# Decoder layer: three output tiles of the projection's middle part issued behind attention's last value product, and other slots for the last part's loads

## The chip, the cores and the metric

One core of a Trainium2 chip runs the whole program. Its engines work side by side, each in its own order: TensorE (PE in the profile, its weight loads PEld), VectorE (DVE), ScalarE (ACT), GpSimd (POOL) and SyncE (SP), which issues most DMAs. The metric is device time in microseconds of one execution; a median over several runs is given.

## The reference

One layer of a causal decoder, for 1024 prompt tokens and 8 sequences of 8 new tokens (N = 1088 columns, D = 1024):

```python
h = rms_norm(x, norm_mix_g)
proj = h @ w_in                       # conv branch a, and q, k, v of 12 heads of 64
a = silu(layer_norm(depthwise_conv(glu(proj)), ...))          # width 31
o = attend(q, k, v)                   # dilated windows (128,1), (512,4), (2048,16), merged
x = x + concatenate([a, o]) @ w_out   # the output projection: 1024 x 1024
h = rms_norm(x, norm_ffn_g)
x = x + (silu(depthwise_conv(h @ w_gate)) * (h @ w_up)) @ w_down
y = rms_norm(x, norm_final_g)
```

Outputs are y for prompt and new tokens, the keys and values, and the convolution states. All of it is float32; the change touches the line of `w_out` and what stands before and behind it.

## The kernel before

Activations lie with channels on the 128 partitions and the 1088 tokens along the free side, so that an operand is eight tiles of 128 x 1088. Every float32 factor is split in a high part (rounded by a ScalarE copy) and a low part (the difference, by VectorE or GpSimd), and a product is three matmuls: high x high, high x low, low x high (`gemm`, L188 to L190; `block_product`, L951 to L954).

**Order of the work.** A planner simulates the engines while the program is built and writes each engine's order: of the instructions that are ready in its simulation, the one that stands first in the program is taken. `tc.issue_after(ins)` binds an instruction behind another one on the same engine, without a wait on any other engine; `high_priority` moves instructions forward. On the chip each engine follows its written order strictly, so one that waits holds up all behind it. SyncE's DMA queue is such an order too.

**Attention.** `prompt_heads` goes through the 12 heads, each in two halves `u`. `scores` (L673 matmuls, L677 masks and row minima on VectorE) is followed by `weighted` of the half before: exponentials (L714, ScalarE), transposes of the weights (L741, into two PSUM banks `t`, copied to SBUF at L745 and L747), and value products (L762) that sum in one PSUM tile `o`; they stand in the list `done`. L765 copies one half of the result; `turned_out[0]` is that copy. `normalise` ends a pair of heads: sums are exchanged (L651), turned (L778) and multiplied (L780, the tile `cat`), and stored to DRAM in `mixed`. The cached sequences go through `sample_attention` in between.

**Output projection in three parts.** `PARTS = (3, 3, 2)` splits the 1024 input channels. The first part (conv branch and the first attention tile) and the middle part (three attention tiles) are `out_part`: for each of eight output tiles m, weights are loaded (`load_w`: raw load L157, high part L161 on ScalarE, low part L163 on GpSimd; two raw buffers, five buffers for parts), `gemm` runs over the three input tiles, and the result is added to `x2[m]` (L890, VectorE) from two PSUM banks. TensorE takes these matmuls wherever attention leaves it free. `ORDER = (4, 5, 6, 7, 0, 1, 2, 3)` and `DEFER = 3`: for tiles 4, 5 and 6 the middle part makes only the first 544 columns, and the other 544 are deferred to the last part.

**The last part.** It contracts the last two attention tiles, in two column halves of 544 (`out_half(0)`, `out_half(1)`), with four PSUM pairs of two banks. Its memory is the pool F, laid over the pools of attention and of the parts before; each tag of F has eight slots of 544 columns, and a load into a slot waits for the readers of what lay there. Its loads run in one chain on SyncE (`queued` and `load_input`, each behind `last_load`), its ScalarE conversions in one chain behind `turned_out[0]` (`last_high`). Before the change the loads come in this order: input 0 of half 0, raw weights of four output tiles (two loads), input 0 of half 1, raw weights of the other four, weights of the three deferred tiles, four raw gate weights, the three deferred inputs, input 1 of half 1, four raw up weights. Input 1 of half 0 is not loaded but made from `cat` in SBUF (L921, L922). The low parts of half 1's two inputs are made on VectorE (L1016), all others by GpSimd (L1003), and `lows_made` keeps the last of them: the first residual add (L1174), and through it all others of half 0, is issued behind it. Each tile of half 0 is one product of 12 matmuls of 272 columns; then its residual add, a store to DRAM (L1176), a square (L1179) and the sum of squares (L1183). Half 1 does the deferred product too for its first three tiles. Then come the norm, the scaling (L1188) and the first products of the feed-forward net, which holds the time from about 605 us to the end.

## Time and profile before

| | us |
|---|---|
| median of 3 runs | 1336.86 (1335.79 to 1343.06) |
| profiled execution | 1336.84 |
| its span, first to last instruction | 1335.1 |
| TensorE busy in the span | 1293.8 |
| VectorE, ScalarE, GpSimd busy | 936.4, 561.0, 472.5 |
| mean granted TensorE clock | 0.989 |

The span is what the profile shows of one execution. "Busy" of TensorE counts its pipelined matmuls, each until its end, so starts of successive matmuls lie closer than their durations. The granted clock is the share of full speed that the throttle allowed. Times in rows count from the span's start. A row of a timeline gives start, length, engine, line, operation, operands, and in brackets the idle time before it with what ended it.

### The profile page before, as it was taken

The numbers are of one execution on the slowest core, as the hardware profiler recorded it, in microseconds if no ns is written. First come the engines' busy times: TensorE is split into PE (matmuls) and PEld (weight loads), VectorE is DVE, ScalarE is ACT, GpSimd is POOL, SyncE is SP. The second block draws the span as 40 slices with busy tenths as digits, with TensorE's granted clock in tenths as the row PEclk, the third lists the DMA queues.
The fourth block names the chain that finished last, engine by engine and source line by source line (L and its number), as shares of the span: only waits on it lengthen the run. The fifth ranks groups of instructions, "written<-read, shape, count | busy, mean of one in ns | idle before, by whom it ended". The sixth has DMA issues, their size and how long they took to land.

```text
span 1335.1 us, 26004 instructions
## 1 busy us (share of the span) xinstructions
PE 1293.8 (97%) x10322; PEld 1253.4 (94%) x10322; DVE 936.4 (70%) x1793; ACT 561.0 (42%) x1130; POOL 472.5 (35%) x387
## 2 busy tenths in 40 slices
PE   9999999999999999889999999999999999999996
PEld 9999988999978879788999999999999999999996
DVE  7478879565575677468977677676776659967656
ACT  7321221547584564454633233333333344334432
POOL 0121112111011125321647556464565544445610
PEclk9999999999999999889999999999999999999999
DMA  9248677564799985351023231332313395352412
GB/s 328 59 169 290 245 268 206 166 167 118 216 285 290 311 273 161 102 209 47 32 91 123 91 122 48 108 122 91 121 35 121 100 356 194 108 180 92 156 41 95
DMA packets 93658, 211.43 MB, mean 158 GB/s; under 512 B 13920, under 2 KB 42720, under 8 KB 93536
## 3 DMA queue, kind: packets, MB, share of 16 engines
q1 hardware_dynamic: 92960, 209.02, 47.8%
q8 instruction: 81, 1.33, 0.4%
q10 hardware_dynamic: 576, 0.75, 0.2%
q14 instruction: 41, 0.34, 0.1%
HBM read 153.69 MB, written 56.04 MB: 157 GB/s over the span
## 4 chain that ended last, share of the span: by engine, by line
PE 83%; DVE 10%; DMA 4%; issue 2%; ACT 0%; SPq 0%; DVEq 0%; ACTq 0%
PE g L188 6%; PE g L190 6%; PE g L189 6%; PE g L951 5%; PE g L954 5%; PE g L953 5%; PE py L951 5%; PE py L953 5%; PE py L954 4%; PE px L954 3%; PE pz L953 3%; PE pz L951 3%; PE pz L954 3%; PE px L953 3%; PE px L951 3%; PE s L673 3%
## 5 line engine op out<-in xcount | busy, mean ns | idle before, releaser
L163 POOL TENSOR_TENSOR wl<-wr,wh 128x1024 fp32r<-128x1024 f32 (+1 forms) x34 | 60.1, 1769 | 307.2 <-PE g L190 175.5
L188 PE MATMUL g<-xh,wh 128*128 128x384 f32 (+1 forms) x472 | 157.0, 333 | 1.3 <-DVE qkv L469 0.7
L190 PE MATMUL g<-xh,wl 128*128 128x384 f32 (+1 forms) x472 | 155.4, 329 | 0.0
L189 PE MATMUL g<-xl,wh 128*128 128x384 f32 (+1 forms) x472 | 155.3, 329 | 0.0
L951 PE MATMUL g<-ux,as 128*128 128x272 f32 x504 | 145.2, 288 | 0.4 <-DVE x L1584 0.4
L954 PE MATMUL g<-ux,as 128*128 128x272 f32 x504 | 145.4, 289 | 0.0
L953 PE MATMUL g<-ux,as 128*128 128x272 f32 x504 | 144.8, 287 | 0.0
L1102 POOL TENSOR_TENSOR wb<-wr,wb 128x512 fp32r<-128x512 f32 x79 | 115.0, 1465 | 54.0 <-ACT wb L1101 54.0
L1494 POOL TENSOR_TENSOR as<-ar,as 128x640 fp32r<-128x640 f32 (+1 forms) x56 | 92.1, 1654 | 101.4 <-ACT as L1493 90.5
L1101 ACT ACTIVATE wb<-wr 128x512 fp32r<-128x512 f32 x79 | 49.6, 628 | 160.6 <-DVE wr L1136 102.9
L951 PEld LDWEIGHTS g<-ux,as 128*128 128x128 f32 x504 | 95.1, 189 | 0.8 <-issue 0.8
L954 PEld LDWEIGHTS g<-ux,as 128*128 128x128 f32 x504 | 94.9, 188 | 0.0
L953 PEld LDWEIGHTS g<-ux,as 128*128 128x128 f32 x504 | 94.7, 188 | 0.0
L714 ACT ACTIVATE y<-y,m 128x128 f32<-128x128 f32 (+1 forms) x192 | 88.5, 465 | 12.4 <-DVE m L702 11.5
L188 PEld LDWEIGHTS g<-xh,wh 128*128 128x128 f32 x472 | 88.8, 188 | 3.7 <-issue 2.1
L1362 DVE SCALAR_TENSOR_TENSOR fc<-gb,prm,fc 128x1104 f32<-128x1104 f32 x44 | 80.5, 1851 | 14.8 <-ACT fc L1360 14.4
L189 PEld LDWEIGHTS g<-xl,wh 128*128 128x128 f32 x472 | 88.9, 188 | 0.2
L190 PEld LDWEIGHTS g<-xh,wl 128*128 128x128 f32 x472 | 88.9, 188 | 0.0
L415 DVE SCALAR_TENSOR_TENSOR cacc<-gp,prm,cacc 128x1024 f32<-128x1024 f32 x60 | 85.0, 1416 | 0.1
L1102 POOL TENSOR_TENSOR wa<-wr,wa 128x512 fp32r<-128x512 f32 x40 | 54.6, 1366 | 79.4 <-ACT wa L1101 79.4
L677 DVE CUSTOM_DVE_ANT_0 y<-s,pmk 128x128 f32<-128x128 f32 (+1 forms) x192 | 63.7, 376 | 26.1 <-PE s L673 23.4
L161 ACT ACTIVATE wh<-wr 128x1024 fp32r<-128x1024 f32 (+1 forms) x36 | 29.6, 822 | 116.2 <-PE g L190 91.9
(399 smaller groups left out, 4316.6 us busy)
## 6 DMA issues: line engine op xcount, KB each, us to landing
cr<-in_kc SPq DMA_DIRECT2D x24, 768.0 KB, 8.3
cr<-in_vc SPq DMA_DIRECT2D x24, 768.0 KB, 7.9
ux<-ub SPq DMA_DIRECT2D x63, 272.0 KB, 4.0
kk<-dk SPq DMA_DIRECT2D x48, 256.0 KB, 5.6
wr<-in_w_in SPq DMA_DIRECT2D x20, 512.0 KB, 5.4
wr<-in_w_gate SPq DMA_DIRECT2D x20, 512.0 KB, 3.3
wr<-in_w_up SPq DMA_DIRECT2D x20, 512.0 KB, 4.5
ub<-u SPq DMA_DIRECT2D x18, 544.0 KB, 3.7
```

Of the source, the lines that this page charges most:

```text
L188: nc.tensor.matmul(ps[c], whi[:, k, :], xh[:, t0:t0 + n], start=(k == 0), stop=False)
L189: nc.tensor.matmul(ps[c], whi[:, k, :], xl[:, t0:t0 + n], start=False, stop=False)
L190: nc.tensor.matmul(ps[c], wlo[:, k, :], xh[:, t0:t0 + n], start=False, stop=(k == nk - 1))
L415: eng.scalar_tensor_tensor(acc[:, :S], gp[:, j:j + S], col(w0 + j), acc[:, :S], op0=ALU.mult, op1=ALU.add)
L677: nc.vector.tensor_tensor_reduce(out=y[:, o:o + n], in0=ps[:, o:o + n], in1=mask, op0=ALU.add, op1=ALU.min, scale=1.0, scalar=3e38, accum_ ...
L714: nc.scalar.activation(y, y, AF.Exp, bias=m[:, 4 * g + i:4 * g + i + 1], scale=-1.0, accum_out=den[:, g, 2 * hd + u, i:i + 1])
L951: nc.tensor.matmul(ps, whi[:, k, :], xh[:, t], start=(start and k == 0), stop=False, skip_group_check=True)
L953: nc.tensor.matmul(ps, whi[:, k, :], xl[:, t], start=False, stop=False, skip_group_check=True)
L954: last = nc.tensor.matmul(ps, wlo[:, k, :], xh[:, t], start=False, stop=(stop and k == nk - 1), skip_group_check=True).ins
L1102: nc.gpsimd.tensor_sub(lo, x, hi.bitcast(F32))
L1362: nc.vector.scalar_tensor_tensor(c[:, :W], gb[i][:, t:t + W], col(C_FW + 3 * f + t), c[:, :W], op0=ALU.mult, op1=ALU.add)
L1494: nc.gpsimd.tensor_sub(lo, raw, hi.bitcast(F32))
```

## The change

- `weighted` keeps its last value product in `weighed[0]`. In the middle part, the matmuls of output tiles 5, 6 and 7 (`m >= KT - BEHIND`) are issued behind it; the evictions are not bound.
- The last part's raw weights are loaded into slots of tag `b11` in place of `t1`; the low parts of these weights go to `t3` in place of `b21`, except the first pair's.
- The three deferred inputs are loaded (and converted) ahead of the deferred tiles' weights and the gate weights, and their raw and low tile lies in `b21`, in place of `t3`.
- `lows_made` is gone. The two low parts of half 1's inputs are kept in `late_lows` and made on VectorE behind the third and the fourth residual add of half 0, and the first residual add of a half is bound to nothing.

```diff
+BEHIND = 3
@@ weighted
                             done.append(nc.tensor.matmul(dst, v, m, start=first, stop=(left[x] == 0)).ins)
                         o += w
+            weighed[0] = done[-1]
@@ out_part
-                gemm(w, part, n, ev, chunks=CHUNKS if k0 == 0 or m not in ORDER[:DEFER] else HALF)
+                with tc.issue_after(weighed[0]) if k0 and m >= KT - BEHIND else nullcontext():
+                    gemm(w, part, n, ev, chunks=CHUNKS if k0 == 0 or m not in ORDER[:DEFER] else HALF)
@@ load_input
-        part, lows_made = [[], []], []
+        part, late_lows = [[], []], []
...
-            lows_made.append((nc.vector if h else nc.gpsimd).tensor_sub(lo, raw, hi.bitcast(F32)).ins)
+            if h:
+                late_lows.append((lo, raw, hi))
+            else:
+                nc.gpsimd.tensor_sub(lo, raw, hi.bitcast(F32))
@@ weights of the last part
-                raw = slot("t1", "wr", F32, 2 * n * P)
+                raw = slot("b11", "wr", F32, 2 * n * P)
...
-                hi, lo = early["b21"].pop() if early["b21"] else slot("b21", "wh", w=512), slot("b21", "wl", w=512)
+                hi, lo = early["b21"].pop() if early["b21"] else slot("b21", "wh", w=512), slot("b21" if m0 == ORDER[0] else "t3", "wl", w=512)
@@ deferred inputs, now ahead of the two loops below
-        for m in ORDER[:DEFER]:
-            queued(raw_wd[m], w_out[m, :, kd * P:k0 * P])
-        gate_raw = [slot("t1", "wr", F32, D // 2) for _ in range(4)]
-        for i, r in enumerate(gate_raw):
-            queued(r, w_gate[i // 2 * HF][:, i % 2 * (D // 2):(i % 2 + 1) * (D // 2)])
         for i in range(n1):
-            hi, lo = slot("t3", "mh"), slot("t3", "ml")
+            lo, hi = slot("b21", "ml"), slot("t3", "mh")
             raw = lo.bitcast(F32)
             queued(raw, mixed[kd + i][:, HN:])
...
+        for m in ORDER[:DEFER]:
+            queued(raw_wd[m], w_out[m, :, kd * P:k0 * P])
+        gate_raw = [slot("t1", "wr", F32, D // 2) for _ in range(4)]
+        for i, r in enumerate(gate_raw):
+            queued(r, w_gate[i // 2 * HF][:, i % 2 * (D // 2):(i % 2 + 1) * (D // 2)])
@@ out_half
-                earlier = rooted[0] if h and j == 1 else residuals[-1] if residuals else lows_made[-1]
-                with tc.issue_after(earlier):
+                earlier = rooted[0] if h and j == 1 else residuals[-1] if residuals else None
+                with tc.issue_after(earlier) if earlier else nullcontext():
                     residuals.append(nc.vector.tensor_add(x, all_of(ps), x).ins)
+                if not h and j > 1 and late_lows:
+                    lo, raw, hi = late_lows.pop(0)
+                    with tc.issue_after(residuals[-1]):
+                        nc.vector.tensor_sub(lo, raw, hi.bitcast(F32))
```

## The prediction

> **What bounds the kernel now.** I read the page's first lines, then TensorE's waits around the change, then that stretch cut into pieces, and last the instructions at the edges of the pieces. From the page:

> ```profile
> span 1335.1 us, 26004 instructions
> ...
> PE 1293.8 (97%) x10322; PEld 1253.4 (94%) x10322; DVE 936.4 (70%) x1793; ACT 561.0 (42%) x1130; POOL 472.5 (35%) x387
> ```

> TensorE is busy 97% of the span, so only its 41 us of idle time, and the time in which its clock is slow, can be won. Its waits between 535 and 600 us (what waited for what: total, times, longest):

> ```profile
> PE g L951 <- DVE x L1174: 5.9, 1, 5.9
> PE g L951 <- ACT wh L1002: 2.9, 1, 2.9
> PE t L778 <- DVE db L775: 2.3, 1, 2.3
> ```

> These 11.1 us lie between the end of attention and the last part of the projection, more than a quarter of all idle time. The pieces below run from the first matmul of tile 5 of the middle part to the end of the last part's first column half (length, busy time of PE, PEld, DVE, ACT, POOL with instructions, granted clock, DMA share, GB/s):

> ```profile
> 540.96:555.75 14.79, 14.79 (x126) 13.88 (x124) 7.22 (x17) 5.85 (x18) 2.02 (x2) 1.00 0.14 45
> 555.75:562.21 6.46, 1.28 (x10) 0.83 (x9) 3.08 (x4) 4.05 (x8) 2.02 (x3) 0.88 0.72 235
> 562.21:570.98 8.77, 8.69 (x48) 8.25 (x48) 1.63 (x1) 2.16 (x4) 6.28 (x5) 0.70 0.85 252
> 570.98:576.98 6.00, 0.10 (x1) 0.03 (x1) 1.99 (x3) 4.64 (x9) 3.99 (x3) 0.78 0.80 310
> 576.98:584.95 7.97, 7.97 (x48) 7.97 (x49) 7.87 (x11) 4.15 (x8) 3.78 (x4) 0.74 0.90 307
> ```

> Together 43.99 us. Attention's tail is full (14.79 of 14.79); then TensorE is nearly empty twice (1.28 of 6.46, 0.10 of 6.00), and in the two pieces of work behind these holes the granted clock is 0.70 and 0.74. Nine matmuls of 272 columns at full clock:

> ```profile
> 540.96 0.28 PE L188 MATMUL g<-mh,wh 128*128 128x272 f32 x1
> ...
> 541.96 0.29 PE L190 MATMUL g<-mh,wl 128*128 128x272 f32 x1
> ```

> From start to start that is 1.00/8 = 0.125 us. The last part's first half has 2 x 48 of them, 12.0 us at this pace against 8.77 + 7.97 = 16.7, so 4.7 us go to the clock.

> **The change, part by part.** *The wait on the late low part.* Why 5.9 us (ScalarE, then VectorE):

> ```profile
> 572.26 2.04 ACT L1002 ACTIVATE mh<-ml 128x544 fp32r<-128x544 f32 x3 [7.84 <-DMA ml<-mixed]
> ```

> ```profile
> 574.99 1.21 DVE L1016 TENSOR_TENSOR ml<-mx,mh 128x544 fp32r<-128x544 f32 x1 [10.11 <-ACT mh L1015]
> 576.12 2.60 DVE L1174 TENSOR_TENSOR x<-g,x 128x544 f32<-128x544 f32 x4
> ```

> All residual adds are issued behind the low part of the second half's last input (L1016). That waits for its high part, which ScalarE makes behind three conversions (L1002) that wait 7.84 us for loads. Four tiles fill the four PSUM pairs, nobody empties them, and the fifth tile waits. The change drops this order and puts VectorE's two low parts behind the third and the fourth add. What is late next: a late low would hold up only adds five to eight, so TensorE could still do all eight tiles. VectorE's load fits: eight adds, seven square sums, two lows and four low parts of gate weights, 21 instructions of about 2.60/4 = 0.65 us, are 13.7 us beside 12 of matmuls, and only the adds free PSUM. So the 5.9 us and the slow clock behind them go.

> *Loads and slots.* Count and bytes of the DMAs stay. SyncE's queue waited, between 535 and 575:

> ```profile
> SPq L1025 <- PE t L741: 10.7, 1, 10.7
> ...
> SPq L1025 <- DMA mixed<-cat: 5.3, 2, 3.9
> SPq L1025 <- PE o L762: 3.5, 1, 3.5
> ```

> The first raw weight load waits 10.7 us for transposes that read the memory under its slot, the next 3.5 for value products, and everything else in this queue stands behind them. As I read the pools, the new slots lie where the readers are scores and cache products, which end before 540. The three deferred inputs also move ahead of three weight loads and four gate loads, so the 7.84 us before 572.26 should go. The conversions stay chained behind the copy of attention's output, so none starts before attention ends: the earlier loads gain nothing by themselves, and if they came late they would cost up to the 7.84 us again. The gate and weight loads that are moved back I cost at nothing; the first half's 12 us of products cover them.

> *The three tiles.* Tiles 5 and 6 have 18 matmuls of 272 columns each, tile 7 has 18 of 384 and 9 of 320.

> ```profile
> 548.38 0.33 PE L188 MATMUL g<-mh,wh 128*128 128x384 f32 x1
> ...
> 549.79 0.34 PE L190 MATMUL g<-mh,wl 128*128 128x384 f32 x1
> ```

> 384 columns take 1.41/8 = 0.176 us, 320 by columns 0.147: 36 x 0.125 + 18 x 0.176 + 9 x 0.147 = 9.0 us. They leave attention's tail, where they filled TensorE's free time, and go behind the last value product, where 5.2 us (2.3 + 2.9) are free. The tail's own work is 14.8 - 9.0 = 5.8 us, so it gets shorter or it shows holes. It gets shorter where attention stood behind these tiles:

> ```profile
> 543.54 0.57 ACT L747 ACTIVATE ph<-t 128x512 f32<-128x512 f32 x1
> ...
> 547.54 0.60 ACT L747 ACTIVATE ph<-t 128x512 f32<-128x512 f32 x1
> 550.60 1.09 ACT L747 ACTIVATE ph<-t 128x512 f32<-128x512 f32 x2 [2.47 <-PE t L741]
> ```

> ```profile
> 545.10 0.43 PE L762 MATMUL o<-ph,vw 128*64 128x256 f32 x1
> ...
> 549.97 1.03 PE L741 MATMUL t<-ident,y 128*128 128x128 f32 x8
> ...
> 553.85 0.43 PE L762 MATMUL o<-ph,vw 128*64 128x256 f32 x1
> ```

> The value products at 545.10 could start when the copy ends at 544.11 (0.99 lost), the transposes at 549.97 at 548.14 (1.83), the last value products at 553.85 at 551.69 (2.16): 4.98 us. At full clock the tail is 14.79 - 4.98 = 9.8 us, say 10.1 with handovers; 4.3 of it are holes.

> *New waits.* The first PSUM pair of the last part lies, as I read the pools, on the two banks of the moved tiles, so it waits for tile 7's last eviction:

> ```profile
> 553.95 0.49 DVE L890 TENSOR_TENSOR x<-g,x 128x320 f32<-128x320 f32 x1 [0.76 <-PE g L190]
> ```

> Bounds: 0, if a free pair is taken, and 0.49 + 0.76 = 1.25; I take 0.8. GpSimd makes tile 7's low weights only when tile 5 frees a buffer, and the low part of attention's last output is queued behind; tiles 6 and 7 (6.7 us) cover both. Without cover each costs an instruction of 1 to 1.5 us; bounds 0 and 2.5, I take 0.7, since the cover is long.

> *The clock.* What it does after thin stretches:

> ```profile
> 553.80:557.20 3.40, 2.60 (x31) 2.15 (x30) 1.49 (x3) 1.27 (x2) 0.00 (x0) 1.00 0.28 92
> ...
> 618.60:622.05 3.45, 1.99 (x17) 1.71 (x17) 2.18 (x10) 1.74 (x5) 0.00 (x0) 1.00 0.00 0
> 622.05:625.40 3.35, 3.35 (x17) 3.35 (x16) 3.35 (x5) 2.88 (x7) 1.99 (x2) 0.51 0.02 5
> ```

> 3.45 us with 1.99 busy were followed by 3.35 us at 0.51 of the clock; after 2.60 busy in 3.40 the transposes still ran at full clock. In the thinned tail 5.8 of 10.1 us are busy, about 2 in 3.4: right at the edge. If the clock falls there, value products and transposes double (the tail's 5.8 us, of which some 4 lie on its chain), and the moved tiles run at half pace until it comes back, after 3 to 5 us (2.5 more). Lost: 0 to 6.5 us. I take 3.2, the middle, since the rows stand on both sides.

> [...]

> **The sum** is made against the profiled execution (1336.84 us: its span 1335.1 and 1.74 around it; the median of the runs, 1336.86, is the same). Before: 43.99. After: tail 10.1 + transposes of the normalisation 1.3 + moved tiles 9.0 + PSUM 0.8 + handovers 0.7 + first half 12.0 + clock 3.2 = 37.1. Saved 6.9 us: **1329.9**. Behind 585 all shifts along: VectorE, which was busy 7.87 of the last 7.97 us, starts its adds earlier by as much as TensorE.

> **Rivals.** *Warm tail:* the clock holds. For it: 2.60 in 3.40 held. Against: 4.3 us of holes. Saved 6.9 + 3.2 = 10.1: 1326.7. *Cold tail:* slow from the first hole into the moved tiles; 6.5 lost in place of 3.2. Saved 3.6: 1333.2. *It doesn't do what it says:* the planner's order moves the holes into the tail (9.0 us, no shortening), 5.2 are filled behind it, and the 5.9 become a wait for the second half's inputs: 9.0 - 5.2 - 4.7 of clock, and as much clock lost in the tail: 1336 to 1338. Against: the 4.98 us are delays in one engine's order. *GpSimd held up by VectorE* is the case on the other side:

> ```profile
> L1334 POOL COPY gb<-sft x22: 193/1179/8857, 642.9 to 1023.5; 128x16 f32<-128x16 f32 x22
> ```

> ```profile
> L1003 POOL TENSOR_TENSOR ml<-ml,mh x3: 1337/1337/1832, 573.0 to 575.6; 128x544 fp32r<-128x544 f32 x3
> ```

> (ns, least, median, most.) GpSimd now makes most low parts while VectorE has little to do (1.63 of 8.77 us). After the change they run beside the adds. One tiny copy took 8.86 us in place of 0.19. If a low part of the deferred inputs is held like that, some 3 us of lead are used up first: 8.9 - 3 + 1.7 of slow clock (half of 3.35) = 7.6 us lost, 1337.5; two holds lose 16.5, 1346.4. It decides once GpSimd is more than 10 us behind (lead and gain together). Against: beside a VectorE that was busy too, the lows took at most 1.83 in place of 1.34.

> **How the numbers follow.** Forecast (4.7 to 8.5 saved) 0.42; warm tail 0.20; cold tail 0.17; no effect 0.06; one hold 0.05; two holds 0.10. Half a per cent, 6.7 us, is about what a measurement of this kernel tells from no change. Faster by more: the warm tail and 0.30 of the forecast's 0.42, 0.50. Same: 0.12 + 0.17 + 0.06 + 0.05 = 0.40. Slower: 0.10. The forecast's own range is 1328.3 to 1332.1; the range for 8 in 10 goes from 1325.5 (warm tail, no PSUM wait and few handovers) to 1337.5 (one hold).

> **What would show it.** Right: 63 matmuls of L188 to L190 behind the last L762; no wait of L951 on L1174; the last value products 2 to 5 us nearer to tile 4's end; the first half's 96 matmuls within 13 us. For the clock: 1.00 granted in the tail and the moved tiles (warm) or near 0.5 (cold). Wrong: a wait of L951 on L1003, or a first half that starts after 568 although the tiles moved.

## The result, and the profile after

The changed kernel takes 1326.28 us (median of 4 runs, 1325.62 to 1327.05) beside 1339.96 us for the kernel before (median of 4 runs, 1335.79 to 1345.11). The ratio is **0.9896, 95% interval 0.9854 to 0.9938**. Measured again, 1327.1 beside 1340.25, it is 0.9904 (0.9882 to 0.9927). The profiled execution took 1326.0 us, its span 1324.2; the one of before had a span of 1335.1. The profiles to be compared therefore differ by 10.9 us.

From the first lines of the page of the changed kernel:

```profile
span 1324.2 us, 26004 instructions
...
PE 1291.0 (97%) x10322; PEld 1248.9 (94%) x10322; DVE 939.3 (71%) x1793; ACT 561.1 (42%) x1130; POOL 473.7 (36%) x387
```

The work is the same (26004 instructions). In the changed kernel line numbers moved by one to ten: the residual add is now L1180 (it was L1174), the projection's matmuls L189 to L191, the last part's L954 to L957, the value product L763. TensorE's waits between 535 and 700 us (what waited for what: total, times, longest):

```profile
PE t L742 <- ACT y L715: 0.8, 2, 0.7
PE s L652 <- DVE xe L649: 0.8, 1, 0.8
PE t L742 <- ACT ph L748: 0.8, 1, 0.8
PE o L763 <- ACT ph L748: 0.7, 1, 0.7
PE g L954 <- DVE x L892: 0.7, 1, 0.7
```

The waits of 5.9, 2.9 and 2.3 us are gone, and what came instead are six waits, none over 0.8 us and 3.8 us together. The pieces of that stretch (length, busy time of PE, PEld, DVE, ACT, POOL with instructions, granted clock, DMA share, GB/s) are attention's tail, the moved tiles, the last part's first half, and the way to the first gate product (the first matmul of the feed-forward net, L970 of the kernel before):

```profile
540.41:552.25 11.84, 8.60 (x62) 6.16 (x60) 4.12 (x10) 5.82 (x18) 1.00 (x1) 0.86 0.43 141
552.25:563.08 10.83, 10.16 (x74) 9.92 (x72) 6.39 (x11) 6.12 (x11) 5.34 (x6) 1.00 0.24 76
563.08:575.38 12.30, 12.30 (x98) 12.30 (x99) 8.71 (x11) 7.05 (x13) 9.54 (x8) 1.00 0.99 337
575.38:596.41 21.03, 20.87 (x165) 20.44 (x165) 19.29 (x36) 12.00 (x23) 2.66 (x2) 1.00 0.55 207
```

The first half, 8.77 + 7.97 us of work at clocks of 0.70 and 0.74 before, with 6.00 us of waiting between, is now one full piece of 12.30 us at clock 1.00. The first three pieces are 34.97 us; before, the same way took 43.99, or 44.16 when its last matmul too is counted to its end, as here.

**A common start.** Up to tile 3's last nine matmuls (320 columns) the order of work is the same in all kernels below, but this point lies at 533.6 to 540.6 us in the profiles, with identical work ahead of it. So all kernels are compared from there. For the kernel before (536.62) and the changed one (536.07) the 10.9 us split into 0.55 ahead of this point, 9.19 from it to the end of the first half (48.50 to 39.31 us), -0.52 from there to the first gate product (20.51 to 21.03), and 1.7 behind it (729.5 to 727.8).

### The profile page after: what moved, and what is told of

Its sections match the earlier page's. It is cut to its first block, busy times and chain, and to the rows that moved or that the text cites. A ratio compares the mean times of both kernels' runs of the same rounds, so it can differ in the third digit from the quotient of the medians.

```text
span 1324.2 us, 26004 instructions
## 1 busy us (share of the span) xinstructions
PE 1291.0 (97%) x10322; PEld 1248.9 (94%) x10322; DVE 939.3 (71%) x1793; ACT 561.1 (42%) x1130; POOL 473.7 (36%) x387
## 4 chain that ended last, share of the span: by engine, by line
PE 77%; DVE 14%; DMA 5%; ACT 2%; issue 2%; SPq 0%; DVEq 0%; ACTq 0%
PE g L189 6%; PE g L191 6%; PE g L190 6%; PE py L954 4%; PE py L957 4%; PE py L956 4%; PE g L954 4%; PE g L957 4%; PE g L956 4%; PE pz L954 3%; PE pz L957 3%; PE pz L956 3%; PE px L954 3%; PE px L956 3%; PE px L957 3%; PE o L763 3%
## 5 line engine op out<-in xcount | busy, mean ns | idle before, releaser
L189 PE MATMUL g<-xh,wh 128*128 128x384 f32 (+1 forms) x472 | 157.0, 333 | 1.2 <-DVE qkv L466 1.2
L191 PE MATMUL g<-xh,wl 128*128 128x384 f32 (+1 forms) x472 | 155.3, 329 | 0.0
L190 PE MATMUL g<-xl,wh 128*128 128x384 f32 (+1 forms) x472 | 155.2, 329 | 0.0
L954 PE MATMUL g<-ux,as 128*128 128x272 f32 x504 | 145.1, 288 | 0.4 <-DVE x L1594 0.4
L957 PE MATMUL g<-ux,as 128*128 128x272 f32 x504 | 145.4, 288 | 0.0
L954 PEld LDWEIGHTS g<-ux,as 128*128 128x128 f32 x504 | 95.0, 189 | 0.8 <-issue 0.6
L1108 POOL TENSOR_TENSOR wa<-wr,wa 128x512 fp32r<-128x512 f32 x40 | 62.8, 1572 | 91.2 <-ACT wa L1107 91.2
L957 PEld LDWEIGHTS g<-ux,as 128*128 128x128 f32 x504 | 94.8, 188 | 0.0
L715 ACT ACTIVATE y<-y,m 128x128 f32<-128x128 f32 (+1 forms) x192 | 88.5, 464 | 12.4 <-DVE m L703 11.1
L189 PEld LDWEIGHTS g<-xh,wh 128*128 128x128 f32 x472 | 88.7, 188 | 3.1 <-DVE qkv L466 1.8
L190 PEld LDWEIGHTS g<-xl,wh 128*128 128x128 f32 x472 | 88.8, 188 | 0.2
L191 PEld LDWEIGHTS g<-xh,wl 128*128 128x128 f32 x472 | 88.8, 188 | 0.0
```

Source lines behind the costliest of these rows:

```text
L189: nc.tensor.matmul(ps[c], whi[:, k, :], xh[:, t0:t0 + n], start=(k == 0), stop=False)
L190: nc.tensor.matmul(ps[c], whi[:, k, :], xl[:, t0:t0 + n], start=False, stop=False)
L191: nc.tensor.matmul(ps[c], wlo[:, k, :], xh[:, t0:t0 + n], start=False, stop=(k == nk - 1))
L715: nc.scalar.activation(y, y, AF.Exp, bias=m[:, 4 * g + i:4 * g + i + 1], scale=-1.0, accum_out=den[:, g, 2 * hd + u, i:i + 1])
L954: nc.tensor.matmul(ps, whi[:, k, :], xh[:, t], start=(start and k == 0), stop=False, skip_group_check=True)
L957: last = nc.tensor.matmul(ps, wlo[:, k, :], xh[:, t], start=False, stop=(stop and k == nk - 1), skip_group_check=True).ins
```

## The experiments

The table collects what each profile shows, in us: from the start of tile 3's 320-column matmuls to the end of the last part's first half; from there to the first gate product; from there to the span's end; and the number of 3.41 us windows at half clock in each of these stretches (the last section shows how they are read; in the rest those up to 640 us are counted). The last column is the measured ratio to the kernel before, run beside it.

| kernel | to end of first half | to first gate product | rest | slow windows | ratio (95%) |
|---|---|---|---|---|---|
| before | 48.50 | 20.51 | 729.5 | 4, 0, 1 | 1 |
| changed, first profile | 39.31 | 21.03 | 727.8 | 1, 0, 0 | 0.9896 (0.9854 to 0.9938) |
| changed again (base_after) | 37.70 | 21.02 | 728.2 | 0, 0, 0 | 0.9904 (0.9882 to 0.9927) |
| tiles_only | 47.23 | 20.51 | 731.4 | 3, 0, 1 | 1.0006 (0.9984 to 1.0027) |
| order_only | 40.99 | 25.33 | 727.2 | 2, 1, 0 | 0.9971 (0.9951 to 0.9992) |
| loads_only | 48.13 | 20.56 | 730.2 | 4, 0, 1 | 1.0026 (1.0005 to 1.0047) |
| order_and_loads | 40.81 | 24.52 | 728.7 | 2, 1, 0 | 0.9947 (0.9924 to 0.9969) |
| tiles_and_order | 37.70 | 24.38 | 727.7 | 0, 1, 0 | 0.9945 (0.9930 to 0.9960) |
| behind_1 | 39.03 | 22.04 | 727.7 | 1, 0, 0 | 0.9937 (0.9920 to 0.9954) |
| behind_2 | 37.53 | 22.10 | 728.4 | 0, 0, 0 | 0.9924 (0.9900 to 0.9947) |
| behind_4 | 37.09 | 23.16 | 727.9 | 0, 1, 0 | 0.9915 (0.9899 to 0.9930) |
| warm_matmul | 37.75 | 21.68 | 728.0 | 0, 0, 0 | 0.9908 (0.9884 to 0.9932) |
| warm_transpose | 37.73 | 23.59 | 727.9 | 0, 1, 0 | 0.9928 (0.9906 to 0.9949) |
| tail_copy | 35.17 | 25.09 | 728.3 | 0, 2, 0 | 0.9890 (0.9867 to 0.9912) |

The rows from tiles_only to order_and_loads were measured on one chip, those from tiles_and_order to behind_4 on a second, base_after and the last three on a third.

### The three parts, one at a time and in pairs

The change has three parts that can stand alone: the three tiles behind the last value product, the order of VectorE's adds and late low parts, and the loads with their slots.

```
tiles:   weighed[0] = done[-1]                    # in weighted
         with tc.issue_after(weighed[0]) if k0 and m >= KT - BEHIND else nullcontext(): gemm(...)
order:   earlier = ... residuals[-1] if residuals else None   # was: lows_made[-1]
         two low parts on VectorE behind the third and the fourth add
loads:   raw = slot("b11", "wr", ...)             # was: "t1"; low parts in "b21" and "t3"
         deferred inputs queued ahead of the deferred and the gate weights
```

Tiles alone:

> Kernel before, and only the three tiles moved behind the last value product. My theory (the parts interlock): the holes of 2.3 and 2.9 us behind attention are filled and the last part's first half starts near 563 at full clock, but its fifth tile still waits for the late low part, which comes only as much earlier as attention ends earlier (3 to 4 us): a wait of L951 on L1174 of 3 to 5 us stays; saved 3 to 5.5 us (1331 to 1334 where the kernel before takes 1336.9). Rival (the parts add up): the fill alone takes holes and slow clock away, 7 to 9 us saved.

Order alone:

> Kernel before, and only the order on VectorE changed (no add behind the last low part, the two late lows behind adds three and four). My theory: the 5.9 us wait and the slow clock behind it go; the holes of 2.3 and 2.9 us and the slow clock behind them stay; the second half then waits 1 to 3 us for GpSimd's low parts of the deferred inputs, whose loads still come at 572; saved 5 to 7.5 us. Rival (the early loads are the cause): 2 us or less saved, TensorE waits for the loads in another place.

Loads alone:

> Kernel before, and only slots and order of the last part's loads changed. My theory: the adds still stand behind the late low, whose input is loaded behind the store of attention's last output; saved 0 to 2 us, the wait of L951 on L1174 stays over 4 us. Rival (the early loads are the cause): 5 us or more saved.

Order and loads, without the tiles:

> The changed kernel without the moved tiles (bound to none). My theory: holes of 5.2 us behind attention and about 2.4 us of slow clock stay, everything else as in the changed kernel; saved 6 to 8.5 us, so the moved tiles are worth 2 to 5 us on top. Rival (the fill is the main part): saved under 5 us.

Tiles and order, without the loads:

> The changed kernel with slots and order of the loads as before. My theory: the loads gain little by themselves; deferred inputs come some 4 us later than in the changed kernel, and the second half waits 0 to 3 us for their low parts or for the sums on VectorE; 7 to 11 us saved. Rival (the slots are what lets order and tiles pay): a wait of over 4 us stays, under 6 us saved.

Alone, the tiles change nothing that is measured, the order gains 0.3%, and the loads come out 0.3% slower; all three together gain 1.0%. That the loads alone cost something isn't shown: the interval hardly leaves 1, and their profile is 0.4 us shorter to the end of the first half, 0.7 longer behind the gate, and 2.8 later at the common start, where the work is still the same. Against what was expected: the tiles alone were to save 3 to 5.5 us and saved none; the order alone saved its 5 to 7.5 us up to the end of the first half, but 3.9 in time; the two pairs came within their ranges (7.1 and 7.4 us by their ratios), though order and loads lose 3.5 us between the first half and the gate that weren't expected. The tiles alone do fill the two holes after attention, but what they save goes into the wait that the kernel before already had, as TensorE's waits of that kernel show (5.9 us before):

```profile
PE g L954 <- DVE x L1177: 6.9, 1, 6.9
```

So neither the tiles nor the loads alone win anything while the residual adds keep their old order; tiles and loads together without it were not run. The order alone takes 7.5 us out of the way to the end of the first half (48.50 to 40.99), the tiles behind it another 3.3 (to 37.70), the loads next to none there (0.37 alone, 0.18 beside the order, 0.00 beside the other two). But order alone gives 4.8 of its 7.5 back before the first gate product (20.51 to 25.33). Two of TensorE's waits in order_only, and two windows of it (length, PE busy, granted clock, DMA share, GB/s):

```profile
PE g L210 <- DVE sq L1190: 1.9, 1, 1.9
PE g L954 <- POOL wl L1003: 0.9, 1, 0.9
```

```profile
587.38:590.79 3.41, 1.51 (x13) 1.00 0.88 318
590.79:594.21 3.42, 3.42 (x18) 0.50 0.01 2
```

The earlier adds bring TensorE to the root's sums (L210: matmuls with a single column, which add up the squares for the norm) before VectorE's squares are there, the stretch becomes thin, and 3.4 us at half clock follow. With tiles and order the same happens at another place: TensorE waits 1.3 us for GpSimd's low part of weights, and half clock follows that too:

```profile
PE g L957 <- POOL wl L1006: 1.3, 1, 1.3
```

```profile
575.92:579.33 3.41, 1.78 (x12) 1.00 1.04 406
579.33:582.74 3.41, 3.41 (x16) 0.50 1.05 387
```

With the loads this wait is gone (21.02 us in place of 24.38). In this pair of profiles that is what the loads are worth: 3.4 us between the first half and the first gate product, none ahead of it. About half of it is the slow window (3.41 us at half clock); beside the order alone, where a slow window stays, the loads gain 0.8 us there (25.33 to 24.52).

### How many tiles

```
-BEHIND = 3
+BEHIND = 1      # behind_1; 2 in behind_2, 4 in behind_4
```

> The changed kernel with only tile 7 (4.5 us) behind the last value product; tiles 5 and 6 fill attention's tail again. My theory (a filler in the tail costs only what it delays attention by, and TensorE's order there has 2.8 us of such delays for tiles 5 and 6): tail about 12.6 us with 2.3 us of holes and full clock, 4.5 us of tile 7 behind it, first half from about 560: from tile 4's end to the end of the first half 31 to 34 us (changed kernel 35.0), so 9 to 13 us saved against the kernel before. Rival (three tiles are needed to cover the gap until the last part's parts are made): a hole of 2 to 4 us before the first half and slow clock in it; 5 to 8 us saved.

> The changed kernel with tiles 6 and 7 (6.75 us) behind; tile 5 fills the tail. My theory: tail about 10 to 11 us with 2 to 3 us of holes, 6.75 us behind, no hole before the first half; 31 to 34 us from tile 4's end to the end of the first half; 10 to 13 us saved. Rival: same as the changed kernel or 1 to 3 us slower than it.

> The changed kernel with tiles 4 to 7 (11.25 us) behind. My theory: the tail loses another 2.25 us of filler where nothing of attention stood behind it, so it shows that much more hole, and its clock is slow for longer; 1 to 4 us slower than the changed kernel, 6 to 9 us saved. Rival (behind is the better place for any tile): the same as the changed kernel or faster.

To the first gate product the four kernels lie between 58.72 (three tiles, second profile) and 61.07 us (one), and the intervals of their ratios overlap, so no order among them is shown. With one tile behind, the hole after it stays (3.3 us of waits for ScalarE's weights, and 3.4 us at half clock); with two the rest of the hole is 2.0 us; with three it is 0.7. The thin tail gets fuller in return. Two of the moved tiles do nearly all in these profiles. Of the expectations, the rival was right for one tile (the hole and the slow clock stay); two tiles take 33.2 us from tile 4's end to the end of the first half, within 31 to 34, but with a hole that wasn't expected; four tiles are no slower than three, as their rival said.

### Keeping the tail's clock up

Fourteen more matmuls, or as many transposes, of 128 columns, whose output nobody reads, between the last exponentials:

```
 for t in ts:
-    nc.tensor.transpose(pt[:, o:o + P], t, ident)
+    turn = nc.tensor.transpose(pt[:, o:o + P], t, ident).ins
+    for _ in range(fills.get(o, 0)):          # last head, first group: behind its 2nd and its 4th transpose
+        with tc.issue_after(turn):
+            turn = nc.tensor.matmul(fill[:, :P], onesc, onesc, start=True, stop=True).ins
+            # warm_transpose: nc.tensor.transpose(fill[:, :P], onesc, ident)
```

> The changed kernel as it stands, beside the next three, so that all four are measured on one chip. Both theories: the ratio near 0.990 again; from tile 4's end to the end of the last part's first half 35.0 us, with the 3.4 us behind tile 4's end thin (1.7 busy) and the 3.4 us behind these at 0.53 of the clock.

> The changed kernel with 14 more matmul instructions of 128 columns that compute nothing, in the two gaps of 0.66 and 0.81 us between the exponentials and the last exchange: they fill some 1.5 us in which TensorE waits anyway. My theory, the clock term is the thin 3.4 us and nothing else: the next 3.4 us run at full clock, the twelve value products take 1.7 in place of 3.1 us, and 1.0 to 1.6 us are saved against the changed kernel, all in this tail. Rival, the slow clock comes from something else in the tail (its tiny tiles, or the DMA that begins there): it stays near 0.5, and the kernel is 0 to 0.5 us slower than the changed one.

> The same with 14 transposes of 128 columns in place of the 14 matmuls, in the same two gaps, of the same length. If transposes count for the clock as matmuls do: as the kernel with the matmuls, full clock and 1.0 to 1.6 us saved. [...]

What was to be compared isn't there, since the unchanged copy did not repeat its slow window: in base_after the same thin tail ran on at a granted clock of 1.00, with the first of its twelve value products in 0.43 us, where it took 0.69 in the first profile. The two fills neither gain nor lose there (37.75 and 37.73 beside 37.70); behind it the kernel with transposes has a slow window at the root's sums (23.59). Whether transposes hold the clock can be read from the windows themselves. Two windows of warm_transpose (length, PE busy, granted clock, DMA share, GB/s):

```profile
543.93:547.34 3.41, 3.12 (x23) 1.00 0.89 280
547.34:550.75 3.41, 2.64 (x23) 1.00 0.63 212
```

In the first of them the 14 added transposes were busy for 1.86 us and attention's four (L744) for 1.09, partly at the same time; the other five matmuls, the last of tile 4 and two of the exchange, were busy for 0.50 us. The next window ran at 1.00. The changed kernel has such a window too, with twelve transposes; below it is the window behind it, and then the transposes of the first alone:

```profile
546.92:550.33 3.41, 1.92 (x14) 1.00 0.02 5
550.33:553.74 3.41, 3.38 (x38) 1.00 0.00 0
```

```profile
546.92:550.33 3.41, 1.75 (x12) 1.00 0.02 5
```

All else in it, the end of two value products, was busy for 0.23 us. Windows with 0.60 us (behind_1) and 1.41 us (tiles_only) of other matmuls and nothing else were followed by half clock. Here, then, transposes held the clock: 1.75 us of them beside 0.23 us of all else, and the next window at 1.00.

### The tail's own order

```
-                if gi in DCOPY[u]:
+                if gi in DCOPY[u] or (p, hd, u, gi) == (NP - 1, 1, 0, 0):
                     nc.vector.tensor_copy(th[:, :o], pt[:, :o])
```

> The changed kernel with one PSUM copy of the last head's first half on VectorE in place of ScalarE, where it stood behind eight exponentials (done at 543.5, its transposes at 539.4); VectorE is idle at that time, and the value products of that half then come before the transposes that they held up. My theory, what is left of the tail is this order on ScalarE and TensorE, not arithmetic: the last value product ends 8.0 to 9.5 us after tile 4's end in place of 11.8, the thin stretch goes, and 2.3 to 4.0 us are saved against the changed kernel. Rival, the last part's loads and conversions set its start: the tail gets shorter, but a wait of the first product on ScalarE's or GpSimd's parts takes 1.5 us or more of it, and 0 to 1.5 us are saved.

To the end of the first half the theory holds: the last value product ends 7.8 us after tile 4's end (8.0 to 9.5 expected), and the stretch takes 35.17 us in place of 37.70, 2.5 saved. What follows takes it back. Two pieces of tail_copy, the same two of base_after, and three windows of tail_copy:

```profile
537.38:572.55 35.17, 33.16 (x265) 31.55 (x264) 22.44 (x41) 21.41 (x48) 16.82 (x15) 1.00 0.57 189
572.55:597.64 25.09, 23.83 (x165) 23.40 (x165) 20.79 (x37) 12.38 (x24) 2.50 (x2) 0.86 0.47 175
```

```profile
535.08:572.78 37.70, 33.78 (x265) 31.55 (x264) 22.24 (x40) 22.12 (x49) 17.05 (x15) 1.00 0.53 181
572.78:593.80 21.02, 20.86 (x165) 20.43 (x165) 19.28 (x36) 11.82 (x23) 2.67 (x2) 1.00 0.55 202
```

```profile
578.60:582.02 3.42, 2.16 (x18) 1.00 0.96 351
582.02:585.43 3.41, 3.41 (x18) 0.50 0.09 33
585.43:588.85 3.42, 3.42 (x17) 0.50 0.21 81
```

In both kernels VectorE is busy some 20 us in the second piece. In tail_copy TensorE arrives at the root's sums earlier than the squares, waits 1.3 us for VectorE (0.2 in base_after), and two windows at half clock follow. The rival named another engine and a place ahead of the first product, where no new wait came (35.17 us, clock 1.00). The median, 1324.65 us beside base_after's 1327.1, is the lowest of all, but the intervals of the two ratios overlap: whether it is better isn't settled.

## Why the prediction was right, and where it was not

The forecast was 1329.9 us, 6.9 saved of 1336.84. Both measurements gave more, 13.7 and 13.2 us between medians, and the profiled pair 10.9. The time lies in the range for 8 in 10, near its warm-tail end, but outside the forecast's own 1328.3 to 1332.1; the ratio that the forecast stands for (0.9948) is outside both intervals. The mechanism was right for the tiles and the adds and wrong for the loads. Of the 4.0 us by which the profiled pair beat the forecast, 2.1 lie in the terms of the sum (34.97 for 37.1). The rest lies ahead of the common start (0.55, with the same work in both, so chance) and behind the first gate product (1.7), less 0.5 lost between; the sum had no term for any of it. How much of the clock term came was chance too, as the two profiles of the changed kernel show.

**The clock in the tail** was the term most mis-sized: 3.2 us (bounds 0 and 6.5). In the first profile it cost 1.6, in the second nothing. The edges of the pieces, TensorE's timeline of the changed kernel:

```profile
540.28 0.28 PE L191 MATMUL g<-mh,wl 128*128 128x272 f32 x1
...
544.02 0.69 PE L763 MATMUL o<-ph,vw 128*64 128x256 f32 x1
...
550.36 0.43 PE L763 MATMUL o<-ph,vw 128*64 128x256 f32 x1 [0.75 <-ACT ph L748]
...
562.09 0.31 PE L191 MATMUL g<-mh,wl 128*128 128x320 f32 x1
563.08 0.36 PE L954 MATMUL g<-mh,wh 128*128 128x272 f32 x1 [0.67 <-DVE x L892]
```

and of base_after:

```profile
539.29 0.28 PE L191 MATMUL g<-mh,wl 128*128 128x272 f32 x1
...
542.81 0.43 PE L763 MATMUL o<-ph,vw 128*64 128x256 f32 x1
...
547.74 0.43 PE L763 MATMUL o<-ph,vw 128*64 128x256 f32 x1 [0.75 <-ACT ph L748]
```

One value product takes 0.69 us in the one, 0.43 in the other. The last ones start 9.9 us (550.36 - 540.41) and 8.3 us (547.74 - 539.42) behind tile 4's end, which is the last of these rows with 272 columns; before it was 12.9 (553.85 - 540.96). So they came 2.9 and 4.6 us nearer, within the 2 to 5 of the prediction. The tail is 11.84 us in the first profile and 1.6 less, 10.2, in the second: the 10.1 of the prediction's sum, without any clock term. Its warm tail and its middle are the same kernel in two executions, in which the windows cut the tail differently: see the last section. That slow clock would last 3 to 5 us was the author's estimate; in the first profile it lasted 3.42 us, in the kernel before 6.84 after the first hole and 6.84 after the second (560.64 to 567.48 and 574.29 to 581.13).

**The wait on the late low part.** Right as written. VectorE's timeline of the changed kernel:

```profile
565.61 0.72 DVE L1180 TENSOR_TENSOR x<-g,x 128x544 f32<-128x544 f32 x1 [2.68 <-PE g L957]
...
572.89 0.71 DVE L1180 TENSOR_TENSOR x<-g,x 128x544 f32<-128x544 f32 x1
573.52 2.17 DVE L1184 TENSOR_TENSOR ml<-mx,mh 128x544 fp32r<-128x544 f32 x2
575.62 0.71 DVE L1180 TENSOR_TENSOR x<-g,x 128x544 f32<-128x544 f32 x1
```

The late lows came late, and they held up adds behind the sixth only, where TensorE had its free pairs. The step counted the squares into VectorE's 13.7 us, but held that only the adds bind, since they free PSUM; that the squares are due at the root's sums it left out. In the changed kernel TensorE waits 0.2 us for them, of the 0.5 that are lost between the first half and the gate in the table (the rest isn't traced); where the kernel gets there sooner, in tail_copy, it is 1.3 and two slow windows.

**Moved tiles, PSUM wait, handovers.** From 552.25 to 562.40 the two transpose groups and the three tiles take 10.15 us (predicted 1.3 + 9.0); the PSUM wait is the predicted one, 0.67 us for 0.8. The 0.7 for handovers isn't there: TensorE waits for no part of GpSimd's in this stretch. The first half took 12.30 us for 12.0.

**Loads and slots.** This step was wrong in its reason, and its value of nothing was wrong too. SyncE's queue in the changed kernel, and ScalarE's conversions:

```profile
SPq L1031 <- DMA mixed<-cat: 19.2, 2, 16.2
```

```profile
564.79 1.32 ACT L1005 ACTIVATE mh<-ml 128x544 fp32r<-128x544 f32 x2 [1.94 <-DMA ml<-mixed]
566.86 0.66 ACT L1005 ACTIVATE mh<-ml 128x544 fp32r<-128x544 f32 x1 [0.75 <-DMA ml<-mixed]
...
572.72 0.66 ACT L1018 ACTIVATE mh<-mx 128x544 fp32r<-128x544 f32 x1 [1.50 <-DMA mx<-mixed]
```

The queue no longer waits for readers of the old slots, but it stands as long behind the store of attention's output. The 7.84 us of ScalarE became 4.19, not nothing. The loads help later, at the deferred weights' low parts (1.3 us of waiting and a slow window less, by the comparison of tiles_and_order with base_after). Why a weight load waits for that store wasn't traced.

**Behind the first half.** "All shifts along" missed two changes: 0.5 us lost on the way to the gate, and 1.7 gained further on. The kernel before had half clock at 622 us, behind the thin 3.45 us at 618.60 that the prediction quoted; all kernels with the new order of adds have none there, and those without it all have one.

**The rivals.** The warm tail is what one of the two profiles shows. Neither a hold of GpSimd nor the cold tail came: GpSimd's low parts of the deferred inputs took 1.37 to 1.86 us each, and the moved tiles ran at a clock of 1.00. The case "it doesn't do what it says" has the time of the tiles alone (1.0006) but not their way: there the tail gets as short as in base_after, and the adds' wait takes it back.

## What to carry to other kernels

Fill holes and remove waits that share one stretch together, and judge them together: here the loads, the tiles and the order gained -0.3, 0 and 0.3% alone, and together 1.0%; what the tiles saved went into the next wait, and much of what the order saved into a wait and the clock further on. Look for the wait that ends last first (here the adds behind a late conversion); work moved into holes ahead of it gained nothing. After such a gain, ask which engine the next fixed point needs: here VectorE's squares at the root's sums took back what the shorter tail had won.

## What the runs showed of the hardware

```profile
557.23:560.65 3.42, 0.63 (x4) 1.00 0.81 269
560.65:564.06 3.41, 1.77 (x6) 0.50 0.61 172
564.06:567.47 3.41, 3.41 (x17) 0.50 0.88 246
567.47:570.89 3.42, 3.42 (x29) 1.00 0.92 296
570.89:574.30 3.41, 0.19 (x2) 1.00 1.05 408
574.30:577.71 3.41, 0.73 (x3) 0.50 0.41 156
577.71:581.13 3.42, 3.42 (x17) 0.50 1.09 319
```

Every turn to half clock that is looked at here stands behind a window that is thin (0.19 to 1.85 us busy) or holds one-column sums (below). A full window shows 29 matmuls, one at half clock 17, those that reach over its edges included. The grid lies differently in each execution, so the same hole falls into one window or is split over two. In the changed kernel:

```profile
540.09:543.50 3.41, 1.69 (x9) 1.00 0.90 278
543.50:546.92 3.42, 3.42 (x18) 0.50 0.64 223
```

and in base_after, where tile 4 ends 2.5 us into its window (539.42) and not 0.3 us (540.41):

```profile
540.32:543.73 3.41, 1.95 (x18) 1.00 0.93 296
543.73:547.15 3.42, 2.49 (x19) 1.00 0.29 105
```

So one kernel had one slow window (1.6 us) in one execution and none in the other. Windows with 1.5 us busy and more were followed by half clock too, several of them at the root's sums (1.51 in order_only, 2.16 in tail_copy, 2.64 in behind_4). The fullest, in order_and_loads, has no idle time at all, but 18 such one-column sums (L210) fill 2.05 us of it:

```profile
39.42:42.83 3.41, 3.41 (x28) 1.00 0.02 5
42.83:46.24 3.41, 3.41 (x14) 0.50 0.00 0
```

Of the windows at full clock without one-column sums, in the kernel before and the changed one from 15 to 1310 us and in the other 12 profiles from about 499 to 640 us, every one with at most 1.41 us busy was followed by half clock and none with more than 1.85; in between there are both (1.55 held in order_only, 1.69 fell in the changed kernel). With such sums, the window above included, eight were followed by half clock, at 1.51 to 3.41 us; in warm_matmul one with 2.83 was not. The thin stretch at 618.60 from which the prediction took its edge holds eight such sums beside its transposes. Why windows with these sums fell at more busy time than the others wasn't shown. In the kernel before TensorE was busy for 1.77 + 3.41 + 0.73 + 3.42 us of the four slow windows above and for 3.41 of the one at 622 us. As an estimate, half of these 12.7 us, some 6.3, went to the clock, 1.6 or nothing after: about half of the whole gain.
